# A decoder trunk on one core: retention states in four tiles per burst, gating behind the output product, the last squares as parts of their own

## The chip, the cores and the metric

The kernel runs on one core of a Trainium2 chip. The metric is the time of one execution in device microseconds; it is given as the median of several runs. A profile is one further execution, with its own time beside its span (first to last instruction).

## The reference

One inference step of two decoder layers on 256 prompt tokens and 8 x 4 sample tokens (288 columns), in fp32, model width 2048. Layer 0 mixes by pooling and spatial gating, layer 1 by retention; each is followed by a gated FFN of width 5632 with a causal convolution. A norm stands before and after each sub-layer:

```python
        x = x + rms_norm(m, norm_mix_post[l])
        h = rms_norm(x, norm_ffn_pre[l])
        ...
        x = x + rms_norm(f, norm_ffn_post[l])
```

Retention has 8 heads with a key width of 256 and a value width of 512. For each sample sequence it reads and writes a state of 256 x 512 per head:

```python
        o = jnp.einsum('bhij,bjhe->bihe', sc, vc) + jnp.einsum('bihd,bhde->bihe', qc, S) * xi[None, :, :, None]
        S = g_c[None, :, None, None] * S + jnp.einsum('bjhd,bjhe->bhde', kc * zeta[None, :, :, None], vc)
```

The head's output is normalised, multiplied by a gate silu(h w_g) and put through the output product w_o. The states are outputs too.

## The kernel before

**Weights and products.** All weights come as one stream of 867 chunks of 128 x 1024 (eight blocks of 128 x 128). A chunk is loaded on the SP queue (line 126, tile raw, three buffers), cast by ACT into a high part (L135, whi) and split by DVE into a low part (L144, wlo), four buffers each. A block is used by one group of three matmuls (mm3: L204, L206, L209), with the activations also split into a high and a low part. `product` runs groups over the contracted blocks for each output block and calls an evacuation at its end.

**Side work.** Everything else is written as Python generators in four lists ("evac", "fast", "late", "slow"). After every group `tick` lowers each list's counter by one; at zero the head of the list takes its next step and sets the counter by the number that it yields. So `yield 24` means that the next step is recorded some 24 groups later. The order of every engine's instructions is fixed by this; a list can also be driven to its end at once (`step` in a loop, `drain`).

**Retention.** For head h: `head` (q, k, v products, 128 groups), `gates` (64 groups), and products of the output for earlier heads (`out_part`). When the last v block is evacuated, `units` joins the list "slow". It handles the head's sample states in four bursts n (even or odd sequences, first or second half of the key width), each on four sequences of 128 x 512. A burst loads the states (`load_state`, L873, on SP, one DMA of 1 MB into the single tile s0), and after `yield 24` issues four matmuls of q with the state (L890, qi_ps), in the last burst a product with the own tokens (L893), and four products of k and v (L896, sn_ps). DVE updates the four states (L899), and POOL issues one DMA that stores the tile (L902). The next load follows 16 groups later (12 in the last head) and must wait for that store, since there is one tile. After the last burst the product is normalised (`normed`: statistics on DVE L923 to L415, a power on POOL L417, tile lr, the result "on" on DVE L928), transposed by TensorE (L910, ot_ps), multiplied by gn and the gate, and split into rhi and rlo, the input of `out_part`. `gates` of the next head begins its first evacuation by driving "slow" until the head before it is through.

**Statistics.** `add_out` evacuates the last part of an output product. `squared` squares each of the 16 blocks on ACT; POOL sums blocks 1 to 14 into tile sqm (L322); block 15 stays a part of its own (L408, sqt). `rms_stat` sums each part over the partitions by three small matmuls (L299, st_ps), with keep-warm matmuls (L279) or, in the retention layer, the final prompt state (sf_ps) between the parts. DVE (L302) and POOL (L304) make the factor from it, which is broadcast by TensorE (L313).

## Time and profile before

| | |
|---|---|
| median of 3 runs | 2997.86 us (2996.1 to 2997.89) |
| profiled execution | 2991.17 us, span 2989.4 us |
| busy: PE, weight loads, DVE, ACT, POOL | 99%, 97%, 61%, 40%, 11% of the span |
| mean granted clock | 0.997 |
| DMA | 540.27 MB, mean 181 GB/s |

Busy time says how long an engine had an instruction in it. Waits name the engine or DMA that came last before an instruction could start. PEclk is the granted share of TensorE's 2.4 GHz; 0.50 is 1.2 GHz.

### The profile page before, as it was taken

The numbers are of one execution on the slowest core, as the hardware profiler recorded it, in microseconds if no ns is written. First come the engines' busy times: TensorE is split into PE (matmuls) and PEld (weight loads), VectorE is DVE, ScalarE is ACT, GpSimd is POOL, SyncE is SP. The second block draws the span as 40 slices with busy tenths as digits, with TensorE's granted clock in tenths as the row PEclk, the third lists the DMA queues.
The fourth block names the chain that finished last, engine by engine and source line by source line (L and its number), as shares of the span: only waits on it lengthen the run. The fifth ranks groups of instructions, "written<-read, shape, count | busy, mean of one in ns | idle before, by whom it ended". The sixth has DMA issues, their size and how long they took to land.

```text
span 2989.4 us, 53184 instructions
## 1 busy us (share of the span) xinstructions
PE 2953.1 (99%) x21951; PEld 2890.1 (97%) x21951; DVE 1816.9 (61%) x2699; ACT 1209.7 (40%) x1843; POOL 330.5 (11%) x573
## 2 busy tenths in 40 slices
PE   9999999999999999999999999999999999999998
PEld 9999999999999999989999998998999999999998
DVE  6754864665655657656556565676775565565664
ACT  6344434333333345433333343343643433333334
POOL 3503300000000014000000000000600000000003
PEclk9999999999999999999999999999999999999999
DMA  6544455554555554566757756656445455555553
GB/s 235 161 162 150 159 164 172 162 167 165 163 168 165 163 169 155 193 233 220 243 165 240 248 164 239 229 199 236 160 160 170 163 161 171 162 162 173 161 167 129
DMA packets 159283, 540.27 MB, mean 181 GB/s; under 512 B 15968, under 2 KB 21616, under 8 KB 159040
## 3 DMA queue, kind: packets, MB, share of 16 engines
q1 hardware_dynamic: 146720, 493.45, 50.3%
q0 software_dynamic: 11184, 42.38, 4.3%
q8 instruction: 172, 2.82, 0.4%
q10 hardware_dynamic: 1136, 1.04, 0.1%
q14 instruction: 71, 0.58, 0.1%
HBM read 495.20 MB, written 41.60 MB: 180 GB/s over the span
## 4 chain that ended last, share of the span: by engine, by line
PE 89%; DVE 5%; DMA 3%; ACT 1%; POOL 1%; issue 1%; SPq 0%; DVEq 0%; POOLq 0%; ACTq 0%
PE acc_n L204 27%; PE acc_n L209 26%; PE acc_n L206 26%; DVE wlo L144 2%; DMA s<-in_ret_dram 2%; PE acc_h L209 1%; PE acc_h L204 1%; PE acc_h L206 1%; PE qi_ps L890 1%; DMA out_rets_dram<-s 1%; DVE hl L352 1%; DVE s L899 1%; ACT whi L135 0%; PE sn_ps L896 0%; POOL dbl L514 0%
## 5 line engine op out<-in xcount | busy, mean ns | idle before, releaser
L144 DVE TENSOR_TENSOR wlo<-raw,whi 128x1024 fp32r<-128x1024 f32 (+1 forms) x867 | 1065.3, 1237 | 641.8 <-ACT whi L135 635.7
L204 PE MATMUL acc_n<-hh,whi 128*128 128x288 f32 x4368 | 1302.7, 298 | 0.0
L206 PE MATMUL acc_n<-hl,whi 128*128 128x288 f32 x4368 | 1289.7, 295 | 0.0
L209 PE MATMUL acc_n<-hh,wlo 128*128 128x288 f32 x4368 | 1285.9, 294 | 1.6 <-DVE wlo L144 1.6
L135 ACT CAST whi<-raw 128x1024 fp32r<-128x1024 f32 (+1 forms) x867 | 896.7, 1045 | 841.0 <-PE acc_n L206 585.4
L204 PEld LDWEIGHTS acc_n<-hh,whi 128*128 128x128 f32 x4368 | 819.9, 188 | 6.4 <-issue 4.6
L209 PEld LDWEIGHTS acc_n<-hh,wlo 128*128 128x128 f32 x4368 | 823.3, 188 | 2.2 <-DVE wlo L144 2.1
L206 PEld LDWEIGHTS acc_n<-hl,whi 128*128 128x128 f32 x4368 | 821.1, 188 | 1.4
L204 PE MATMUL acc_n<-fhi,whi 128*128 128x288 f32 x1320 | 389.6, 295 | 0.0
L206 PE MATMUL acc_n<-flo,whi 128*128 128x288 f32 x1320 | 389.5, 295 | 0.0
L209 PE MATMUL acc_n<-fhi,wlo 128*128 128x288 f32 x1320 | 388.8, 295 | 0.0
L209 PEld LDWEIGHTS acc_n<-fhi,wlo 128*128 128x128 f32 x1320 | 248.4, 188 | 0.0
L206 PEld LDWEIGHTS acc_n<-flo,whi 128*128 128x128 f32 x1320 | 247.7, 188 | 0.0
L204 PEld LDWEIGHTS acc_n<-fhi,whi 128*128 128x128 f32 x1320 | 247.4, 187 | 0.0
L632 ACT ACTIVATE gg<-cv 128x256 f32<-128x256 f32 x88 | 36.8, 418 | 372.3 <-DVE cv L630 372.3
L622 POOL COPY co<-fext 128x16 f32<-128x16 f32 x88 | 17.4, 198 | 1419.3 <-DVE fext L620 1419.3
L204 PE MATMUL acc_n<-rhi,whi 128*128 128x288 f32 x496 | 147.4, 297 | 0.0
L206 PE MATMUL acc_n<-rlo,whi 128*128 128x288 f32 x496 | 146.3, 295 | 0.0
L209 PE MATMUL acc_n<-rhi,wlo 128*128 128x288 f32 x496 | 146.2, 295 | 0.0
L899 DVE SCALAR_TENSOR_TENSOR s<-s,sn_ps 128x512 f32<-128x512 f32 x128 | 81.0, 682 | 85.5 <-PE sn_ps L896 85.5
L391 DVE TENSOR_TENSOR mbuf<-mbuf,acc_n 128x288 f32<-128x288 f32 x128 | 57.6, 452 | 113.7 <-PE acc_n L209 113.6
L204 PE MATMUL acc_h<-hh,whi 128*128 128x288 f32 x368 | 109.0, 298 | 1.3 <-ACT whi L135 1.3
(274 smaller groups left out, 2958.9 us busy)
## 6 DMA issues: line engine op xcount, KB each, us to landing
raw<-in_w_dram SPq DMA_DIRECT2D x866, 512.0 KB, 3.6
s<-in_ret_dram SPq DMA_DIRECT2D x32, 1024.0 KB, 6.3
out_rets_dram<-s POOLq DMA_DIRECT2D x32, 1024.0 KB, 5.9
out_retp_dram<-sf POOLq DMA_DIRECT2D x14, 256.0 KB, 2.6
xbuf<-in_x_dram SPq DMA_DIRECT2D x3, 576.0 KB, 6.1
hc<-in_hc_dram SPq DMA_DIRECT2D x8, 177.0 KB, 5.2
out_y_dram<-xbuf SPq DMA_DIRECT2D x3, 288.0 KB, 2.2
out_conv_dram<-co POOLq DMA_DIRECT2D x2, 396.0 KB, 4.1
```

The costliest lines, as they stand in the source:

```text
L135: A.copy(hi[:, a:b], raws[c][:, a:b])
L144: V.tensor_tensor(lo[:, a:b], raw[:, a:b], hi[:, a:b].bitcast(F32), op=ALU.subtract)
L204: PE.matmul(ps, wh, xh, start=start, stop=False)
L206: PE.matmul(ps, wh, xl, start=False, stop=False)
L209: PE.matmul(ps, wl, xh, start=False, stop=stop)
L352: V.scalar_tensor_tensor(hl[k - 2], x[k - 2], col(gain, k - 2), hh[k - 2].bitcast(F32), op0=ALU.mult, op1=ALU.subtract)
L391: V.tensor_tensor(m[:, j, :], m[:, j, :], ps, op=ALU.add)
L622: G.tensor_copy(co[:, f, 0:NB, :], exs[:, :, DS:])
L632: A.activation(g[:, 0:SEQ], c[:, 0:SEQ], AF.Gelu_apprx_tanh)
L890: PE.matmul(pi[32 * g:32 * g + 32, :], qp[:, dt, 32 * b:32 * b + 32], s0[:, g, :], start=n == 0, stop=False, tile_position=(0, 32 * g))
L899: V.scalar_tensor_tensor(s0[:, g, :], s0[:, g, :], g4[h], pns[g], op0=ALU.mult, op1=ALU.add)
```

## The change

The state tile becomes four tiles s0 to s3 of 128 x 512, each with its own load, and its own store as soon as it is updated. The yields change: 20 groups before a head's first burst, 25 before the others (36 in heads 2 and 4), 10 after a burst. The transposes of head h wait until the output product of head h - 2 is recorded. In the statistics, blocks 13, 14 and 15 become parts of their own, in tiles of another tag; the work between parts stands before the last part alone, and without it no keep-warm matmuls stand there.

```diff
--- before.py
+++ after.py
@@ -293,7 +293,7 @@
         zeros = wz.bitcast(F32)
         PE.matmul(ps[0:96, 0:6], zeros[:, 0:96], zeros[:, 0:6], start=True, stop=False)
         for n, sq in enumerate(parts):
-            if n and between:
+            if between and n == len(parts) - 1:
                 between()
             for t in range(3):
                 PE.matmul(ps[0:96, 2 * t:2 * t + 2], sq[:, 96 * t:96 * t + 96], ones[:, 0:2],
@@ -365,7 +365,7 @@
 
     def post_stat(parts, fill=None):
         drain("late")
-        rs = rms_stat(parts, fill[0] if fill else lambda: keep_warm(3))
+        rs = rms_stat(parts, fill[0] if fill else None)
         if fill:
             fill[1]()
         else:
@@ -401,10 +401,10 @@
             if j == 0:
                 parts.append(t288("sqm", tag="sq"))
                 A.activation(parts[0], ps, AF.Square)
-            elif j < KT - 1:
+            elif j < KT - 3:
                 square_add(parts[0], ps, j)
             else:
-                s = t288("sqt", tag="t2")
+                s = t288("sqs", tag="gl")
                 A.activation(s, ps, AF.Square)
                 parts.append(s)
             A.activation(m[:, j, :], ps, AF.Copy, scale=col(gain, j))
@@ -702,7 +702,7 @@
                 return w.rearrange("p t (g c) -> p t g c", c=8)
             return w.rearrange("p (g c) -> p g c", c=8)
         osp = {}
-        rot, tail = [], []
+        rot, tail, projected = [], [], set()
 
         def rope(dst, a, b):
             if not rot:
@@ -846,15 +846,11 @@
                     mm_split(pf, [w[:, jt, 128 * dt:128 * dt + 128] for w in kz], v2[jt], jt == 0, jt == 1)
                 return pf
 
-            last = []
-
             def put_state(dt, pf):
                 if h < HEADS - 1:
                     sf = p1.tile([128, 512], F32, tag="sf", name="sf")
                 else:
-                    if not last:
-                        last.append(p1.tile([128, 4, 512], F32, tag="s0", name="sfl"))
-                    sf = last[0][:, dt, :]
+                    sf = p1.tile([128, 512], F32, tag=f"s{dt}", name="sfl")
                 A.copy(sf, pf)
                 G.dma_start(out=o["retp"][h, 128 * dt:128 * dt + 128, :], in_=sf)
 
@@ -869,25 +865,26 @@
         retsv = o["rets"].rearrange("(g e) h (t p) v -> e h t p g v", e=2, p=128)
 
         def load_state(h, e, dt):
-            s0 = p1.tile([128, 4, 512], F32, tag="s0", name="s0")
-            nc.sync.dma_start(out=s0, in_=retv[e, h, dt])
+            s0 = []
+            for g in range(4):
+                s0.append(p1.tile([128, 512], F32, tag=f"s{g}", name=f"s{g}"))
+                nc.sync.dma_start(out=s0[g], in_=retv[e, h, dt, :, g, :])
             return s0
 
         def units(h, R):
 
 
             qp, km, vs = qpads[h % 2], R["km"], R["vs"]
-            pace = 16 if h < HEADS - 1 else 12
             pi = None
             for n in range(4):
                 e, dt = n % 2, n // 2
                 s0 = load_state(h, e, dt)
-                yield 24
+                yield (36 if h in (2, 4) else 25) if n else 20
                 if pi is None:
                     pi = bank("qi_ps")
                 for g in range(4):
                     b = 2 * g + e
-                    PE.matmul(pi[32 * g:32 * g + 32, :], qp[:, dt, 32 * b:32 * b + 32], s0[:, g, :],
+                    PE.matmul(pi[32 * g:32 * g + 32, :], qp[:, dt, 32 * b:32 * b + 32], s0[g],
                               start=n == 0, stop=False, tile_position=(0, 32 * g))
                 if n == 3:
                     PE.matmul(pi, s2w[h % 2], vs, start=False, stop=True)
@@ -896,14 +893,16 @@
                     PE.matmul(pns[g], km[32 * g:32 * g + 32, e, 128 * dt:128 * dt + 128], vs[32 * g:32 * g + 32, :],
                               start=True, stop=True, tile_position=(32 * g, 0))
                 for g in range(4):
-                    V.scalar_tensor_tensor(s0[:, g, :], s0[:, g, :], g4[h], pns[g], op0=ALU.mult, op1=ALU.add)
+                    V.scalar_tensor_tensor(s0[g], s0[g], g4[h], pns[g], op0=ALU.mult, op1=ALU.add)
+                    G.dma_start(out=retsv[e, h, dt, :, g, :], in_=s0[g])
                     if g == 1:
                         yield 1
-                G.dma_start(out=retsv[e, h, dt], in_=s0)
                 if n == 3:
                     R["on"].append(normed(pi))
-                yield pace
+                yield 10
             on = R["on"]
+            while h >= 2 and h - 2 not in projected:
+                yield 1
             for e in range(4):
                 pt = bank("ot_ps")
                 for t in range(3):
@@ -965,6 +964,7 @@
                 assert step("slow") or ks[-1] in osp
             product([("ret_out", n) for n in ALLK], ks, osp, add_out(heads[0] == 0, parts, "post_mix1"),
                     first=4 if parts is not None else 0)
+            projected.update(heads)
 
         parts = []
         for h in range(HEADS):
```

The order at three places, of before and then of the change.

TensorE at the end of head 0 (qi_ps and sn_ps are the products of a burst, ot_ps the transposes of "on", v_ps a transposed v, acc_n the running product). Before:

```order
L209 MATMUL acc_n<-hh_91,wlo_14263 128x288
L890 MATMUL qi_ps<-s_14308,qpad_12572 32x512 x4
L893 MATMUL qi_ps<-vstk,s2w_12582 128x512
L896 MATMUL sn_ps<-vstk,km 128x512 x4
L910 MATMUL ot_ps<-cst,on 128x128 x12
L204 MATMUL acc_n<-hh_76,whi_14292 128x288
```

Now the burst, and then the place of the transposes:

```order
L887 MATMUL qi_ps<-s_14244,qpad_12572 32x512
L890 MATMUL qi_ps<-vstk,s2w_12582 128x512
L893 MATMUL sn_ps<-vstk,km 128x512 x4
L204 MATMUL acc_n<-hh_77,whi_14254 128x288
...
L807 MATMUL v_ps<-cst,vf 128x128 x2
L808 MATMUL v_ps<-cst,vst_12581 128x128
...
L909 MATMUL ot_ps<-cst,on 128x128 x3
...
L909 MATMUL ot_ps<-cst,on 128x128 x9
L204 MATMUL acc_n<-hh_76,whi_14327 128x288
```

Thirteen groups now stand between the burst and the first three transposes; the other nine follow two groups later, at the place where all twelve stood. From burst to burst it is 39 groups in heads 0, 1, 3, 5, 6 and 7 and 50 in heads 2 and 4; it was 44, and 40 in head 7.

The SP queue around the loads of a burst of head 0 (raw is a weight chunk). Before:

```order
L126 DMA raw_14019<-in_w_dram 128x1024
L873 DMA s_14060<-in_ret_dram 128x4x512
L126 DMA raw_14077<-in_w_dram 128x1024
L126 DMA raw_14127<-in_w_dram 128x1024
L126 DMA raw_14170<-in_w_dram 128x1024
```

Now:

```order
L126 DMA raw_13951<-in_w_dram 128x1024
L871 DMA s_13978<-in_ret_dram 128x512
L871 DMA s_13980<-in_ret_dram 128x512
L871 DMA s_13982<-in_ret_dram 128x512
L871 DMA s_13984<-in_ret_dram 128x512
L126 DMA raw_14015<-in_w_dram 128x1024
```

Four loads stand in the queue ahead of the next weight chunk where one stood.

DVE at the end of head 6 (s is a state tile, bst and mv the statistics of the product). Before:

```order
L727 TENSOR_TENSOR qpad_12574<-qk,hc 128x4x2x4 x2
L144 TENSOR_TENSOR wlo_21516<-raw_21406,whi_21515 128x1024
L899 SCALAR_TENSOR_TENSOR s_21430<-s_21430,sn_ps 128x512 x4
L923 BN_STATS bst_21569<-qi_ps 128x6
L925 BN_AGGR mv_21571<-bst_21569 128x2
L415 TENSOR_SCALAR ve<-mv_21571 128x1
L928 TENSOR_SCALAR on<-qi_ps,mv_21571,lr 128x512
```

Now:

```order
L896 SCALAR_TENSOR_TENSOR s_21594<-s_21594,sn_ps 128x512
L896 SCALAR_TENSOR_TENSOR s_21596<-s_21596,sn_ps 128x512
L144 TENSOR_TENSOR wlo_21691<-raw_21583,whi_21690 128x1024
L896 SCALAR_TENSOR_TENSOR s_21598<-s_21598,sn_ps 128x512
L896 SCALAR_TENSOR_TENSOR s_21600<-s_21600,sn_ps 128x512
L922 BN_STATS bst_21733<-qi_ps 128x6
L924 BN_AGGR mv_21735<-bst_21733 128x2
L415 TENSOR_SCALAR ve<-mv_21735 128x1
L927 TENSOR_SCALAR on<-qi_ps,mv_21735,lr 128x512
```

A weight split now stands between the second and the third update. It is so in heads 3, 5, 6 and 7.

## Rows read from the trace of the kernel before

**Rows 1.** The page, busy time (share of the span) xinstructions of each engine
```profile
PE 2953.1 (99%) x21951; PEld 2890.1 (97%) x21951; DVE 1816.9 (61%) x2699; ACT 1209.7 (40%) x1843; POOL 330.5 (11%) x573
```

**Rows 2.** The waits of TensorE: us in total, times, longest us
```profile
PE qi_ps L890 <- DMA s<-in_ret_dram: 6.4, 7, 1.9
PE ot_ps L910 <- DVE on L928: 5.0, 2, 4.7
...
PE st_ps L299 <- POOL sqm L322: 1.7, 1, 1.7
PE acc_n L209 <- DVE wlo L144: 1.6, 2, 1.0
```

**Rows 3.** The windows: us, busy of PE, PEld, DVE, ACT, POOL; PEclk, DMA share, GB/s
```profile
300.00:1130.00 830.00, 829.32 (x6225) 828.61 (x6224) 494.97 (x684) 330.45 (x453) 60.48 (x161) 1.00 0.52 165
1307.00:1312.00 5.00, 4.92 (x19) 4.63 (x20) 2.93 (x10) 1.30 (x3) 0.00 (x0) 0.50 0.59 195
1605.70:1609.00 3.30, 3.30 (x15) 3.30 (x15) 3.27 (x5) 0.00 (x0) 0.00 (x0) 0.52 0.02 9
2118.00:2124.00 6.00, 5.93 (x36) 5.12 (x37) 1.31 (x4) 1.56 (x4) 2.39 (x5) 1.00 0.31 118
```

**Rows 4.** The timeline of TensorE, end of head 0: start us, us, instruction [idle before]
```profile
1297.66 0.38 PE L807 MATMUL v_ps<-cst,vf 128*128 128x128 f32 x2
...
1300.08 1.07 PE L890 MATMUL qi_ps<-s,qpad 128*32 128x512 f32 x8
...
1301.50 0.50 PE L896 MATMUL sn_ps<-vstk,km 32*128 32x512 f32 x4
...
1307.09 1.33 PE L910 MATMUL ot_ps<-cst,on 128*128 128x128 f32 x5 [4.71 <-DVE on L928]
```

**Rows 5.** The timeline of DVE, the same place
```profile
1298.93 1.22 DVE L144 TENSOR_TENSOR wlo<-raw,whi 128x1024 fp32r<-128x1024 f32 x1
1302.04 2.48 DVE L899 SCALAR_TENSOR_TENSOR s<-s,sn_ps 128x512 f32<-128x512 f32 x4 [1.89 <-PE sn_ps L896]
...
1306.22 0.81 DVE L928 TENSOR_SCALAR on<-qi_ps,mv,lr 128x512 f32<-128x512 f32 x1 [0.68 <-POOL lr L417]
```

**Rows 6.** The timeline of POOL, the same place
```profile
1304.82 0.75 POOL L902 DMA_DIRECT2D out_rets_dram<-s  x1 [18.29 <-DVE s L899]
1305.62 0.56 POOL L417 TENSOR_TENSOR lr<-ve,mhalf 128x1 f32<-128x1 f32 x1
```

**Rows 7.** Lines L873, L902, L859: ns min/median/max of an issue, and its landing
```profile
L873 SPq DMA_DIRECT2D s<-in_ret_dram x32: 378/385/987, 1226.8 to 2067.1; - x32
...
DMA to landing us min/median/max: 5.5/6.3/9.0
...
DMA to landing us min/median/max: 4.7/5.9/8.0
...
L859 POOL DMA_DIRECT2D out_retp_dram<-sf x14: 542/568/613, 1234.7 to 1902.2; - x14
...
DMA to landing us min/median/max: 2.3/2.5/6.2
```

**Rows 8.** The waits of the SP queue: us in total, times, longest us
```profile
SPq L873 <- DMA out_rets_dram<-s: 39.5, 14, 9.0
```

**Rows 9.** The timeline of all engines, the statistic of the first FFN
```profile
1138.79 0.59 PEld L299 LDWEIGHTS st_ps<-ones,sqm 128*96 128x96 f32 x6
...
1139.30 0.54 PEld L279 LDWEIGHTS warm<-wz 128*128 128x128 f32 x3
...
1139.46 0.44 ACT L408 ACTIVATE sqt<-mbuf 128x288 f32<-128x288 f32 x1 [2.44 <-DVE mbuf L394]
...
1139.95 0.66 PEld L299 LDWEIGHTS st_ps<-ones,sqt 128*96 128x96 f32 x6
```

**Rows 10.** The timeline of all engines, the statistic of the retention layer
```profile
2116.02 0.29 PEld L294 LDWEIGHTS st_ps<-wz 128*96 128x96 f32 x2
...
2118.06 0.58 PEld L299 LDWEIGHTS st_ps<-ones,sqm 128*96 128x96 f32 x6 [1.75 <-POOL sqm L322]
```

## The prediction

> **What bounds the kernel now.** I read the page's busy times first: TensorE is busy for 99% of the span [rows 1]. So only two things can shorten the run: less work on TensorE, or fewer of its waits and slow stretches. The change takes away almost no work there: three statistics lose three keep-warm matmuls each, and all four gain six small ones. So the second view is TensorE's waits: state loads cost 6.4 us in seven waits, the transposes behind the normalised product 5.0 us in two, the statistic 1.7 us in one; waits for split weights come to only 1.6 us on that line [rows 2]. These three are what the change touches. Third, the windows with the granted clock: it stands at 0.50 for the 5 us after the longest wait, and at 0.52 for 3.3 us after a wait for a state [rows 3]. 0.50 is the 1.2 GHz level, so half of such a stretch is lost. In a long plain stretch 6225 matmuls take 830 us [rows 3]: 0.133 us each, 0.40 us for the three of a group, which is one step of the side work. I use 0.40 us to turn places in the order into time.
>
> **Part 1: the end of head 0.** Before, the last burst of head 0 is followed at once by all of its twelve transposes, since head 1's first gate forces the side work to its end there. TensorE waits 4.7 us for the tile "on" [rows 2, 4], then runs 5.0 us at half clock [rows 3], which loses 2.5 us: 7.2 us. The wait is a chain: the last state product ends at 1301.50 + 0.50 = 1302.00 [rows 4], then come four updates, the statistics and the power on POOL, and "on" ends at 1306.22 + 0.81 = 1307.03 [rows 5, 6]: 5.03 us. In the new order 13 groups (5.2 us) and a trio of small transposes lie between burst and first gating transposes, because the three periods before it are 39 groups and not 44. 5.2 is over 5.03, so the wait goes and with it the slow clock: -7.2 us. The bound on the other side is 0, if "on" is late for another reason. I take the whole, as the covering work is plain matmuls in fixed order.
>
> **Part 2: state loads and stores in four pieces.** Before, a period is 44 groups, 17.6 us, and a burst of 1.5 us (1.07 for the eight state matmuls, 0.50 for the four products behind them, overlapping a little [rows 4]): 19.1 us. Into it must fit: burst 1.5, updates 2.5 [rows 5], 0.3 to the store's issue (1304.82 less 1304.52) [rows 5, 6], store 5.9, load 6.3 [rows 7]: 16.5 us, and 17.7 where a weight split of 1.22 us [rows 5] stands among the updates. The rest is eaten by the SP queue, where the load stands behind weight loads; 14 of the 32 loads still found the store on its way, 39.5 us in all [rows 8]. So the period is just long enough at the medians, and seven times it was not.
>
> After, a period is 39 groups: 15.6 + 1.5 = 17.1 us (50 groups, 21.5 us, in heads 2 and 4). The slowest piece is the fourth: update ends 4.0 us after the burst's start (5.2 with a weight split), 0.3 to its issue, then a 256 KB store and a 256 KB load. No row has such a piece among three others. The near end is the 256 KB store of the prompt's state, 2.5 us; the far end the worst whole tile, 8.0 for a store and 9.0 for a load [rows 7]. I take 4 us each, nearer to the 256 KB row, since the first three pieces leave earlier: 4.0 + 0.3 + 4 + 4 = 12.3, 13.5 with a split, against 17.1. That leaves 3.6 us for SP. There the load now stands 13 groups (5.2 us) behind the burst instead of 18 or 19, and the weight loads queued behind it wait for the last store; three more issues of 0.385 us [rows 7] add 1.2 us. Those weight loads feed tiles four chunks ahead, and the 1.6 us of waits on split weights [rows 2] show this cover; without it each late us would be one of TensorE. A head's first load stands 21 groups ahead instead of 25: 8.4 us, over the 6.3 median but under the 9.0 worst. For these I keep 1.0 of the 6.4 us: -5.4, and the slow stretch after the 1.9 us wait goes: 3.3 us at 0.52, -1.7. Together -7.1 us (from -8.1, all gone, to the loss of rival 1).
>
> A rule speaks against the pieces. The Trainium skill ("DMA: Bandwidth & Descriptors", section "Anatomy of one DMA") says a DMA costs about 2.0 us fixed plus bytes over 436e3 per us. By it one 1 MB copy takes 4.4 us as an estimate, and four of 256 KB, if each paid in turn, 10.4. The 2.5 us of the 256 KB row agrees with its 2.6 for one piece; whether four overlap no row here shows, and paid in turn they would be rival 1.
>
> **Part 3: transposes closer behind the burst.** Elsewhere 19 groups (15 in head 7) lay between a head's last burst and its transposes; now always 13, 5.2 us. In heads 1, 2 and 4 the chain of 5.03 us fits. In heads 3, 5, 6 and 7 the new order has a weight split between the second and third update: 5.03 + 1.22 = 6.2 us, so TensorE waits 1.0 us in heads 6 and 7, and 0.6 in 3 and 5, where a transposed v (about 0.4 us of TensorE [rows 4]) lies between: 3.2 us. Head 7's old wait, 5.0 - 4.7 = 0.3 [rows 2], goes: +2.9 us. POOL issues four stores, not one, ahead of the power that "on" needs. At 0.57 us, the 256 KB issue [rows 7], the fourth begins 2.8 us after the state products and ends at 3.4, before the power's 3.62 (1305.62 less 1302.00) [rows 6]: nothing. At 0.75, the whole tile's, they run into one another to 4.0 and add 0.4 in each of eight heads. So +0 to +6. The new guard that holds a head's gating until the product two heads back is done delays nothing: the distance is 13 groups in every head, guarded or not.
>
> **Part 4: the last three squares.** In the two FFN statistics and that of layer 0's mixer, the first part's three small matmuls hold the weight port 0.51 us (1138.79 to 1139.30) [rows 9]. Two more parts add 1.02 and end at 1140.32; the last part started at 1139.95 before, right behind its square, which ended at 1139.46 + 0.44 = 1139.90. The keep-warm trio that goes lay under that wait. So +0.37 us, three times: +1.1. In the retention layer the first part waited for POOL's sums until 2118.06 though TensorE was ready at 2116.31 (the zero products of 0.29 from 2116.02); with the last two sums off POOL that is -1.75, and the two parts cost 1.02: -0.7 [rows 10]. Together +0.4 us.
>
> **Sum.** -7.2 - 7.1 + 2.9 + 0.4 = -11.0 us. Against the profiled execution (2991.17 us, of which the span is 2989.4) that is 2980.2. The runs' median lies 6.7 us above that execution; I take the same 11.0 from it: 2986.9 us.
>
> **Rivals.**
> 1. The pieces are as slow as the whole (this is the slower side). The period is now 2 us shorter; if the fourth piece's store and load still take 5.9 + 6.3, the chain is 16.5 to 17.7 us against 17.1, and SP's hold of about 1 us comes on top: 0.4 to 1.6 us of wait in each of the 18 short periods, 7 to 29 us, in place of the old 8.1. Total -7.2 - 8.1 + 2.9 + 0.4 + (7 to 29) = -5 to +17 us, 2993 to 3015. It turns into a loss where the waits pass 12 us in all, 0.67 us a period; by this chain the store and load of the fourth piece must then come to about 11.3 us with a split and 12.5 without. For it: both copies share the engines with the weights, and 14 loads waited for stores [rows 8]. Against: 2.5 us for 256 KB [rows 7], and the early start of three pieces. Chance 0.12.
> 2. The clock falls at the statistics, where the keep-warm trio is gone. Before, the stretch around the retention statistic is at 1.00 although TensorE waited 1.7 us in it [rows 3]. A fall would cost what the two stretches above cost, 1.7 to 2.5 us, at the two statistics that work follows and maybe the third: +3.4 to +7.5, so 2990 to 2994. The Trainium skill ("TensorE: Matmul & The Clock Gate", Part 1) has the clock set by how busy the engine was lately, so that taking filler away invites this. The rows here show falls after waits of 4.7 and 1.9 us and none at the statistic's 1.7, so the trace neither bears it out nor excludes it. Chance 0.12.
> 3. "on" is later than I have it: DVE and POOL are in other work when the burst ends, in most heads, at 1 us more in each: +8, 2995. For it: those engines also carry the splits and evacuations of the running products. Against: before, only head 0 and head 7 waited there at all [rows 2]. Chance 0.11.
> 4. Head 1's forced drain still stalls (nine of its twelve transposes are still issued at the forced place), so the 7.2 us stay: 2994. Against: three go ahead of it. Chance 0.05.
>
> **How the numbers follow.** Forecast 0.60, rivals 0.12, 0.12, 0.11, 0.05. A measurement of this kernel can tell about 0.2%, 6 us, from no change, so faster means below 2991.9. The forecast with its bounds (waits of part 2 all gone and part 3 at 0: 2983; part 3 at its upper end: 2990) lies below that; rival 2 mostly does. Faster: 0.60 + 0.08 = 0.68. Same: rivals 3 and 4, the rest of 2 and half of 1: 0.26. Slower: the upper half of rival 1: 0.06. The range, 2980 to 2996, takes in the forecast's bounds with 3 us for the next run, rivals 2, 3 and 4, and leaves out most of rival 1.
>
> **What would show it.** After: no wait of several us at the transposes of head 0 and the clock at 1.00 there; state waits near 1 us in all; waits of 0.5 to 1 us at the transposes of heads 3, 5, 6 and 7; landing times of the pieces near 4 us; no wait for POOL's sums at the retention statistic, 0.4 us more in each other. The prediction is wrong if pieces land in 6 us or more, if PE's waits for "on" pass 6 us, or if the clock falls at a statistic.

## The result, and the profile after

| | kernel before | changed kernel |
|---|---|---|
| median of the runs side by side | 2994.18 us (6 runs, 2990.11 to 2997.89) | 2979.32 us (6 runs, 2978.10 to 2979.88) |
| ratio, 95% interval | | 0.9949 [0.9937, 0.9962] |
| profiled execution (span) | 2991.17 us (2989.4) | 2978.1 us (2976.3) |

The change is faster by 0.5%. One run of the kernel before, beside experiments 9 to 12, took 5918.56 us and is in no ratio. Three of the six runs of the kernel before are those shown ahead of the prediction (median 2997.86); the other three, taken beside the changed kernel, gave 2990.11 to 2992.27. From profiled execution to profiled execution it is 13.1 us; the forecast's sum was 11.0.

The page, busy time of each engine of the changed kernel:

```profile
PE 2952.5 (99%) x21990; PEld 2890.9 (97%) x21990; DVE 1818.3 (61%) x2699; ACT 1209.7 (41%) x1843; POOL 366.1 (12%) x661
```

TensorE's busy time is where it was [rows 1], 2952.5 us against 2953.1, so nearly all of the 13 us is idle time that went: span less busy time is 23.8 us where it was 36.3. POOL has 35.6 us more, of 96 more DMA issues less the eight sums that went. Next TensorE's waits of the changed kernel, those that stand in [rows 2] and are left:

```profile
PE ot_ps L909 <- DVE on L927: 2.0, 4, 0.7
PE acc_n L209 <- DVE wlo L144: 1.6, 2, 1.0
```

No row for state loads is left (6.4 us in seven waits before). This list has idle time ahead of an instruction; a late piece in the middle of a burst shows instead as a burst that takes longer than its 1.06 us (the first row of head 0 below), and none of the 32 bursts does here. There is no row for POOL's sums at a statistic (1.7 before), and the transposes' wait is 2.0 us in four pieces where it was 5.0 in two. The waits for split weights did not grow. The windows of the changed kernel, with the granted clock in the third column from the right: a plain stretch, the end of head 0, the last statistic.

```profile
300.00:1130.00 830.00, 829.34 (x6225) 828.64 (x6224) 495.49 (x685) 330.10 (x454) 61.51 (x162) 1.00 0.51 165
1300.00:1305.00 5.00, 5.00 (x40) 4.87 (x39) 4.50 (x8) 1.07 (x3) 0.00 (x0) 1.00 0.60 179
...
2960.00:2963.40 3.40, 3.40 (x13) 2.91 (x12) 0.75 (x3) 0.00 (x0) 0.92 (x2) 0.50 0.00 0
```

The plain stretch has 6225 matmuls as in [rows 3]; what changed lies in the retention layer and the statistics. The end of head 0, which ran at 0.50, is at 1.00. The last line is new: at the last statistic the clock stands at 0.50, its 1.2 GHz level, for 3.4 us.

The end of head 0 in the changed kernel, TensorE, then DVE and POOL:

```profile
1293.82 1.06 PE L887 MATMUL qi_ps<-s,qpad 128*32 128x512 f32 x8
...
1295.23 0.51 PE L893 MATMUL sn_ps<-vstk,km 32*128 32x512 f32 x4
...
1301.30 0.49 PE L909 MATMUL ot_ps<-cst,on 128*128 128x128 f32 x3
```

```profile
1295.77 2.48 DVE L896 SCALAR_TENSOR_TENSOR s<-s,sn_ps 128x512 f32<-128x512 f32 x4 [1.31 <-PE sn_ps L893]
...
1299.95 0.81 DVE L927 TENSOR_SCALAR on<-qi_ps,mv,lr 128x512 f32<-128x512 f32 x1 [0.69 <-POOL lr L417]
```

```profile
1296.75 2.33 POOL L897 DMA_DIRECT2D out_rets_dram<-s  x4 [16.30 <-DVE s L896]
1299.35 0.56 POOL L417 TENSOR_TENSOR lr<-ve,mhalf 128x1 f32<-128x1 f32 x1 [0.26 <-DVE ve L415]
```

The state products end at 1295.23 + 0.51 = 1295.74, "on" at 1299.95 + 0.81 = 1300.76: 5.02 us, as before [rows 4 to 6]. The transposes begin at 1301.30, 0.54 us later, with no wait. The four store issues end at 1296.75 + 2.33 = 1299.08, ahead of the power at 1299.35.

Issue (ns, min/median/max) and landing of the state pieces, loads (L871) and stores (L897), and the SP queue's wait at the loads:

```profile
L871 SPq DMA_DIRECT2D s<-in_ret_dram x128: 327/388/1432, 1227.6 to 2048.9; - x128
...
DMA to landing us min/median/max: 3.3/5.1/6.6
...
L897 POOL DMA_DIRECT2D out_rets_dram<-s x128: 539/542/587, 1241.3 to 2061.4; - x128
...
DMA to landing us min/median/max: 2.3/3.0/5.9
```

```profile
SPq L871 <- DMA out_rets_dram<-s: 14.4, 15, 2.4
```

A whole tile's load took 6.3 us and its store 5.9 at the median [rows 7]; a piece's take 5.1 and 3.0. The SP queue's wait for stores fell from 39.5 us, longest 9.0 [rows 8], to 14.4, longest 2.4. By the trace's landing events of all 32 bursts, the last piece lands 0.25 to 7.1 us ahead of its burst, median 3.7; it is less than 1.3 in four of them.

The statistic of the first FFN in the changed kernel, and that of the retention layer behind it:

```profile
1139.35 0.59 PEld L299 LDWEIGHTS st_ps<-ones,sqm 128*96 128x96 f32 x6
...
1139.86 1.61 PEld L299 LDWEIGHTS st_ps<-ones,sqs 128*96 128x96 f32 x18
...
1139.95 0.44 ACT L408 ACTIVATE sqs<-mbuf 128x288 f32<-128x288 f32 x1 [2.45 <-DVE mbuf L394]
...
1145.30 0.40 PE L204 MATMUL acc_h<-hh,whi 128*128 128x288 f32 x1
...
2102.30 0.59 PEld L299 LDWEIGHTS st_ps<-ones,sqm 128*96 128x96 f32 x6
...
2102.82 1.10 PEld L299 LDWEIGHTS st_ps<-ones,sqs 128*96 128x96 f32 x12
```

At the first FFN the three parts follow the first without a gap. In the retention layer the first part follows the zero products at once; its 1.75 us of wait [rows 10] are gone. Measured from the start of the last matmul of the product to the first matmul of the next (to the broadcast of the result for the last one), the four statistics took 5.85, 5.86, 8.37 and 3.35 us before and take 6.15, 6.17, 7.58 and 4.08 after.

### The profile page after: what moved, and what is told of

The parts are those of the page before. It is cut to its first block, busy times and chain, and to the rows that moved or that the text cites. A ratio compares the mean times of both kernels' runs of the same rounds, so it can differ in the third digit from the quotient of the medians.

```text
span 2976.3 us, 53668 instructions
## 1 busy us (share of the span) xinstructions
PE 2952.5 (99%) x21990; PEld 2890.9 (97%) x21990; DVE 1818.3 (61%) x2699; ACT 1209.7 (41%) x1843; POOL 366.1 (12%) x661
## 4 chain that ended last, share of the span: by engine, by line
PE 93%; DVE 4%; ACT 1%; issue 1%; POOL 1%; DMA 0%; SPq 0%; DVEq 0%; POOLq 0%; ACTq 0%
PE acc_n L204 28%; PE acc_n L209 28%; PE acc_n L206 28%; DVE wlo L144 2%; PE acc_h L209 1%; PE acc_h L204 1%; PE acc_h L206 1%; PE qi_ps L887 1%; DVE hl L352 1%; PE sn_ps L893 0%; POOL dbl L514 0%; DVE pn L380 0%; PE st_ps L299 0%; DVE s L896 0%; PE ot_ps L909 0%
## 5 line engine op out<-in xcount | busy, mean ns | idle before, releaser
L897 POOL DMA_DIRECT2D out_rets_dram<-s x128 | 69.4, 542 | 412.7 <-DVE s L896 405.4
```

Source lines behind the costliest of these rows:

```text
L897: G.dma_start(out=retsv[e, h, dt, :, g, :], in_=s0[g])
```

## The experiments

All ratios are to the kernel before, run on the same chip; experiments 1 to 4 shared one chip, 5 to 8 another, 9 to 12 a third. The change itself was run side by side with the kernel before (median 2979.32 us) and in experiment 5 (2978.78); no run of it stands beside experiments 1 to 4 or 9 to 12. The kernel before gave medians of 2991.21, 2991.73 and 2990.09 us in the three groups, so a median may be compared across groups to 1 or 2 us.

### 1. The kernel before, once more

No edit. It tells how large the run-to-run scatter of the base is.

> The kernel before, unchanged, to see how its time, its waits for state loads and its clock spread. Theory A (the first three runs, near 2997, held more or longer waits for state loads, with slow-clock stretches behind them, than the profiled execution with its 6.4 us of such waits): the runs lie between 2989 and 2998, and the ones that take longer show a lower mean clock, by about 0.001 for each 3 us (a 3.4 us stretch at half clock is 0.0006 of the span, and the wait ahead of it is as long); the profile shows the 4.7 us wait at the end of head 0 and between 4 and 13 us of waits for state loads. Rival B (a part of the time that no engine's waits show, such as the launch, differs from session to session): the clock is the same in all runs, and the difference between time and span moves with the time.

Measured: 2991.68 us (11 runs, 2988.6 to 2993.65) beside 2991.21 (28 runs, 2986.94 to 2994.6); ratio 1.0004 [0.9996, 1.0013]. Its profiled execution took 2992.37 us with a span of 2990.7, so 1.7 lie around the span, as in the profile before (2991.17 - 2989.4 = 1.8). The 2996 to 2998 of the three runs ahead of the prediction did not come back here (one single run beside experiments 9 to 12 took 2996.89). Its waits for states were 4.5 us in six, and the wait at the end of head 0 was 4.7 again.

The record has the mean granted clock of 56 runs of this kernel in experiments 1 to 12. The longer a run, the lower its clock: 2987.7 us on average at 0.998 (4 runs), 2989.6 at 0.997 (19), 2991.9 at 0.996 (29) and 2994.3 at 0.995 (4). That is about 2.2 us for each 0.001, where theory A had 3. Between 1.65 and 1.78 us lie around the span in all of them. So theory A holds in this and rival B does not: the scatter lies within the span.

The base of this kernel is 2990 to 2992, and the 6.7 us by which the median shown lay above the profiled execution were not a property of the kernel; what made them is not settled.

### 2. The change with one tile and one store per burst

The rest of the change (yields, guard, statistic) stays.

```diff
-            s0 = []
-            for g in range(4):
-                s0.append(p1.tile([128, 512], F32, tag=f"s{g}", name=f"s{g}"))
-                nc.sync.dma_start(out=s0[g], in_=retv[e, h, dt, :, g, :])
+            s0 = p1.tile([128, 4, 512], F32, tag="s0", name="s0")
+            nc.sync.dma_start(out=s0, in_=retv[e, h, dt])
...
-                    G.dma_start(out=retsv[e, h, dt, :, g, :], in_=s0[g])
                     if g == 1:
                         yield 1
+                G.dma_start(out=retsv[e, h, dt], in_=s0)
```

> The changed kernel with one state tile again (one load, one store of 1 MB), all else as in the change, the yields and with them the order of TensorE included. Theory A (pieces are needed for periods of 39 groups): the chain burst, updates, store 5.9, load 6.3 is 16.5 to 17.7 us against a period of 17.1, with SP's hold on top, so state loads are waited for 7 to 29 us in all, in most of the 18 short periods, and the clock falls behind some: 2988 to 3012, 9 us or more over the change. Rival B (the shorter distance to the gating alone made the gain, the pieces nothing): within 3 us of the change, 2976 to 2982, waits for state loads under 3 us.

Measured: 2984.31 us (11 runs, 2981.72 to 2993.24), ratio 0.9985 [0.9976, 0.9994]. By medians it lies 5.0 to 5.5 us above the change, nearer to rival B's 3 than to theory A's 9; by the ratios 8 to 11. Its runs scatter over 11.5 us, those of the change over 1.8. Its profiled execution was the slowest of its eleven (2993.24), so the waits below are the upper end; the median run, 9 us shorter, left no profile. TensorE's waits there, then the landing of its loads and the SP queue's wait:

```profile
PE qi_ps L889 <- DMA s<-in_ret_dram: 8.8, 6, 3.3
PE ot_ps L911 <- DVE on L929: 2.9, 4, 1.2
```

```profile
DMA to landing us min/median/max: 5.3/6.1/8.3
```

```profile
SPq L873 <- DMA out_rets_dram<-s: 73.4, 24, 6.3
```

With one tile the shorter periods bring the waits for states back, six of them with 8.8 us in this execution, and 24 loads wait 73.4 us for stores. So it is the four tiles that keep the period of 39 groups free of such waits. But by its median this version is still 6.9 us faster than the kernel before: more than half of the gain comes without the four tiles.

### 3. The old distances with four tiles

```diff
-                yield (36 if h in (2, 4) else 25) if n else 20
+                yield 24
...
-                yield 10
+                yield 16 if h < HEADS - 1 else 12
```

> The changed kernel with the yields of before (24 ahead of every burst, 16 behind it, 12 in the last head); four tiles and the new statistics stay. Theory A: all of head 0's transposes stand right behind its last burst again, so the wait of about 4.7 us and the half clock behind it (2.5 us) come back, the waits of 2.0 us for the normalised product in heads 3, 5, 6 and 7 go to 0.3, and the waits for state loads stay at 0 with 44 groups: about +5.5 us to the change, 2983 to 2987. Rival B (the pieces brought nothing, the periods did): waits for state loads return with 4 us or more, 2989 to 2995.

Measured: 2986.82 us (11 runs, 2983.72 to 2988.56), ratio 0.9987 [0.9979, 0.9996]: 7.5 to 8 us above the change by medians, and the upper end of what was expected (5.5). Its waits at the transposes, and the SP queue's at the loads:

```profile
PE ot_ps L909 <- DVE on L927: 5.0, 2, 4.7
```

```profile
SPq L871 <- DMA out_rets_dram<-s: 7.1, 4, 4.8
```

No row for states is in the list, but three bursts were held inside by a late piece, 2.0 us in all. The longest of them, to be read beside the 1.06 us of a burst in the changed kernel:

```profile
1843.50 2.32 PE L887 MATMUL qi_ps<-s,qpad 128*32 128x512 f32 x8
```

Head 0's end costs what it cost before. So Part 1 needs the distances and Part 2 the tiles, but the two are not quite separate: at the old distances four tiles still leave 2.0 us of late pieces, which the expected 5.5 did not have.

### 4. The change with the old statistic

```diff
-            elif j < KT - 3:
+            elif j < KT - 1:
...
-                s = t288("sqs", tag="gl")
+                s = t288("sqt", tag="t2")
```

and the three keep-warm matmuls and their place as before.

> The changed kernel with the statistics of before: blocks 13 and 14 summed on POOL again, three keep-warm matmuls between the parts. Theory A (the new parts gain 0.8 us in the retention statistic and lose 0.3 in each of the other three, 0.4 more in the last where the clock fell): 0.5 us less than the change, that is no difference, 2977 to 2981; the wait of 1.7 us for POOL's sum is back in the retention statistic, each other statistic is 0.3 us shorter, and the clock does not fall at the last statistic. Rival B (the statistics carry a good part of the gain): 3 us or more over the change.

Measured: 2980.33 us (6 runs, 2977.39 to 2983.37), ratio 0.9963 [0.9951, 0.9975], 1.0 above the change. That is within theory A's range, and the new statistic gives nothing that these runs resolve. The profiled execution was the slowest of the six. Two of its bursts were held by late pieces, 1.1 us in all, though tiles and distances are those of the change: their reserve is not whole in every execution. Also in it the wait for POOL's sums is back, and behind it the clock fell for 6.8 us:

```profile
PE st_ps L299 <- POOL sqm L322: 1.7, 1, 1.7
```

```profile
2107.50:2114.30 6.80, 6.80 (x23) 5.58 (x23) 0.16 (x1) 1.17 (x2) 1.43 (x2) 0.50 0.17 64
```

### 5. The changed kernel, once more

No edit; the base for experiments 6 to 8.

> The changed kernel, unchanged, for its spread and as the base of the runs beside it. Theory A (the change made the kernel insensitive to how long a state transfer takes): 2977 to 2982 on any chip, no wait for a state load, while the kernel before lies anywhere between 2987 and 2998. Rival B (the change is as sensitive, and its earlier runs were lucky): single runs scatter by 6 us or more and the profile shows waits for state loads.

Measured: 2978.78 us (5 runs, 2978.57 to 2979.49), before beside it 2991.73 (9 runs, 2986.59 to 2993.56), ratio 0.9959 [0.9945, 0.9972]. By these medians the change is worth 12.95 us.

### 6 and 7. The loads of a head's later bursts 1.6 us later, before and after

Four groups are moved from behind the load to ahead of it, so that TensorE's order and the distance from burst to burst stay. Before (6) and the change (7):

```diff
-                yield 24
+                yield 20 if n else 24
...
-                yield pace
+                yield pace if n == 3 else pace + 4
```

```diff
-                yield (36 if h in (2, 4) else 25) if n else 20
+                yield (32 if h in (2, 4) else 21) if n else 20
...
-                yield 10
+                yield 10 if n == 3 else 14
```

> The kernel before with the loads of a head's second to fourth burst placed four groups (1.6 us) later, at 20 groups ahead of the burst and not 24; the order on TensorE is the same. It imitates state transfers that take 1.6 us longer. Theory A (its loads have no slack, so transfers that take longer on a chip are paid in full): the loads that a store does not already hold back are late by up to 1.6 us more; waits for state loads rise from 4.5 to 6.4 us to 12 to 25, with further stretches at half clock: 5 to 20 us over the kernel before, 2996 to 3011. Rival B (SP's hold behind weight loads decides, not the place): within 3 us of the kernel before.

> The changed kernel with the same shift: the loads of a head's second to fourth burst four groups (1.6 us) later, 21 groups ahead of the burst and not 25 (32 and not 36 in heads 2 and 4); the order on TensorE is the same. Theory A (the pieces have slack): in its trace the last piece landed 0.2 to 7.1 us ahead of its burst, under 1.6 us in five of the 24 places; a shift of 1.6 us then makes waits of about 3 us in all, 1.4 at the longest: 0 to 4 us over the change. Rival B (no slack either): 6 us or more over the change.

Measured: before 3010.09 us (5 runs, 3008.11 to 3012.08), ratio 1.0062 [1.005, 1.0075], 18.4 above the kernel before. The change 2980.74 (5 runs, 2979.59 to 2982.65), ratio 0.9964 [0.9952, 0.9977], 2.0 above experiment 5. Both are what theory A expects. The waits for states in 6; and one of three bursts of 7 (two in head 0, one in head 1) that a late piece held inside:

```profile
PE qi_ps L890 <- DMA s<-in_ret_dram: 16.5, 13, 2.8
```

```profile
1278.14 1.52 PE L887 MATMUL qi_ps<-s,qpad 128*32 128x512 f32 x8
```

The old chain had no reserve: 1.6 us later made thirteen waits of 16.5 us out of seven of 6.4, and its trace has three stretches at half clock in the retention layer besides that at the end of head 0 (3.4, 6.8 and 6.8 us), where the first profile has one. The new one has 1.6 us of reserve in all but five of the 32 bursts (four of the 24 that the shift moves, where the expectation says five), by the change's landing events, although its period is 2 us shorter in 18 of 24 places. The three bursts in 7 took 2.2 us longer than they do unheld, which is the 2.0 that it lost; the list of waits has no row for them.

### 8. A mixed version

The new statistic in the retention layer alone, the other three as before; the last burst's transposes three groups later in the heads where "on" came late.

```diff
-        rs = rms_stat(parts, fill[0] if fill else None)
+        rs = rms_stat(parts, fill[0] if fill else lambda: keep_warm(3))
...
-            elif j < KT - 3:
+            elif j < (KT - 3 if gain == "post_mix1" else KT - 1):
...
-                yield 10
+                yield 13 if n == 3 and h in (3, 5, 6, 7) else 10
```

> The changed kernel with two things put back or moved: the new parts of the statistic in the retention layer alone (the other three statistics as before, with their keep-warm matmuls), and the transposes of heads 3, 5, 6 and 7 three groups (1.2 us) further behind the last burst. Theory A (by the stage times: 0.3 us back in each of three statistics and the clock stays up at the first and last of them, waits of 2.0 us for the normalised product go): 3 us less than the change, 2974 to 2978, the clock at 1.00 from 20 us to the end of the last statistic, waits for the normalised product under 0.5 us. Rival B (the clock at the statistics falls by chance, whatever stands between the parts): within 1.5 us of the change, with a stretch at half clock at one of the statistics.

Measured: 2974.14 us (5 runs, 2974.05 to 2974.69), ratio 0.9943 [0.993, 0.9955]: 4.6 below the change, as theory A expects, so it beats both kernels. No wait for "on" is left. Its statistics take 5.86, 5.86, 7.58 and 3.34 us. The windows of its four parts of the span:

```profile
16.00:300.00 284.00, 280.77 (x2102) 278.45 (x2102) 167.35 (x240) 133.01 (x209) 89.45 (x98) 1.00 0.51 170
300.00:1130.00 830.00, 829.30 (x6225) 828.60 (x6224) 496.44 (x687) 330.78 (x454) 60.67 (x161) 1.00 0.51 165
1130.00:2130.00 1000.00, 997.38 (x7368) 943.28 (x7367) 654.00 (x1072) 410.45 (x721) 157.42 (x238) 1.00 0.63 214
2130.00:2962.00 832.00, 830.26 (x6225) 828.47 (x6223) 485.88 (x678) 325.43 (x444) 55.08 (x158) 1.00 0.50 162
```

The clock is at 1.00 in all four.

### 9 to 12. The mixed version taken apart

Experiment 9 has only the two statistic edits of 8, experiment 10 only the later transposes, experiment 12 is 8 again. Experiment 11 is the change with the keep-warm trio put back (the first edit of 8 alone), all statistics in four parts.

> The change with its new statistic kept in the retention layer alone; the other three statistics as before (one sum for the first parts, three keep-warm matmuls). Theory A (the 4.6 us by which the mixed version beat the change are a sum of a statistic's part and a gating part): the three statistics give back 0.30 + 0.31 + 0.73 = 1.3 us, the waits for the tile on (2.0 us) stay: the change less 1.3, 2977 to 2978 where the change is 2979, and the clock stays up at the last statistic. Theory B (the new statistic costs more than its own path, through the clock): the change less 2.5 or more, 2976.5 or less.

> The change with the transposes of heads 3, 5, 6 and 7 three groups (1.2 us) later, all else as in the change. Theory A: the 2.0 us of waits for the tile on go, nothing else moves: the change less 2.0, about 2977, and the clock still falls at the last statistic. Theory B (nearly all of the mixed version's gain is of the statistics): the change less 0 to 1. Theory C (TensorE's waits in these heads cost more than the profile shows as waits): the change less 3 or more.

> The change with the three keep-warm matmuls put back ahead of the last part in three statistics; the parts stay four. Theory A (the fall of the clock at the last statistic comes from the keep-warm trio that went): no stretch at half clock there, and the trio lies under the wait for the last square or adds up to 0.3 us each: within 1 us of the change. Theory B (the fall comes from the parts, whose small matmuls hold the port for longer): the clock still falls there to half for about 3 us; within 1 us of the change or above it by up to 1.5.

> The mixed version again, beside its two halves. Theory A (its gain over the change is the sum of a statistic's part and a gating part): it lies below the statistic's half by what the gating's half gains, and below the gating's half by what the statistic's half gains, to 1 us; 2974 to 2975.5. Theory B (one of the halves does it all): it lies within 0.7 us of one of them.

| | median us (5 runs each) | range | ratio, 95% interval |
|---|---|---|---|
| 9, statistic alone | 2977.70 | 2976.6 to 2978.58 | 0.9958 [0.9945, 0.9971] |
| 10, gating alone | 2976.63 | 2974.28 to 2979.15 | 0.9953 [0.9938, 0.9968] |
| 11, parts and keep-warm | 2980.18 | 2979.29 to 2981.26 | 0.9967 [0.9954, 0.998] |
| 12, mixed again | 2974.94 | 2973.41 to 2975.17 | 0.9948 [0.9935, 0.996] |

The mixed version lies 2.8 us below 9, which is the gating's worth, and 1.7 below 10, the statistic's worth (1.3 us by the stage times, 0.4 of it the clock). Both halves count, and they add: theory A of these runs. Experiment 10 lies 2.2 to 2.7 below the change, nearer to theory A's 2.0 than to theory C's 3. But by the starts of TensorE's instructions the four waits cost 2.9 us and not the 2.0 of the list (Part 3 below), so theory C's mechanism is there too. One detail of theory A missed: in the profile of experiment 10 the clock did not fall at the last statistic but at the first. In experiment 9 the last statistic runs at full clock again:

```profile
2950.00:2968.00 18.00, 13.68 (x96) 12.36 (x94) 6.99 (x15) 2.81 (x6) 7.17 (x8) 1.00 0.19 70
```

Experiment 11 answers its question in one execution only. With the trio back the clock stayed up at the last statistic, as theory A says; that the trio did it is not shown, since the clock also stayed up there in experiment 10 without it. At the first statistic, which neither theory speaks of, it fell:

```profile
289.10:292.50 3.40, 3.40 (x13) 2.92 (x13) 0.16 (x1) 0.00 (x0) 1.67 (x5) 0.51 0.22 51
```

The trio, which lay under the wait for the last square before, has no cover behind three parts:

```profile
1142.59 1.10 PEld L299 LDWEIGHTS st_ps<-ones,sqs 128*96 128x96 f32 x12
1143.61 0.54 PEld L279 LDWEIGHTS warm<-wz 128*128 128x128 f32 x3
1144.18 0.73 PEld L299 LDWEIGHTS st_ps<-ones,sqs 128*96 128x96 f32 x6
```

The last part starts at 1144.18, 1.59 us after the two before it; in the changed kernel the three follow in one go. At the first FFN that is 0.7 us more than the change by TensorE's starts. The parts and the trio together are the dearest form.

## Why the prediction was right or wrong

The direction was right and the mechanisms were: every wait named in Parts 1, 2 and 4 went. Of its own signs of being wrong one came in full, the clock fell at a statistic (the last); of another there were single cases, load pieces that took up to 6.6 us at a median of 5.1. The time, 2979.3 us, lies 7.6 us below the forecast and 0.7 below the low end.

**The step that failed** is the last of the sum: "The runs' median lies 6.7 us above that execution; I take the same 11.0 from it". The kernel before ran at 2990 to 2992 us everywhere else: 2991.07 (the median of the three runs beside the change), 2991.21, 2991.73 and 2990.09 in the experiments. These lie within about 1 us of the profiled execution, 2991.17, so the 6.7 should have been about 0. The sum against the profiled execution, which the text also gives, was 2980.2; the measured time is 0.9 below it. So most of the miss is a base of three runs, all high, to which a difference from another execution was applied; its range allowed 3 us below the forecast's bounds, less than the 6.7 us by which the base was off.

The rest is in the sizes of the terms, of which Part 2 was the one too small:

- **Part 1, -7.2: right.** No wait at head 0's transposes, clock 1.00 for the 5 us behind them, "on" 5.02 us behind the products (forecast 5.03). Experiment 3 shows the 4.7 us wait whole when the distances alone are put back.
- **Part 2, -7.1: under-sized, -8.1.** The 1.0 us kept for states that still come late was 0. The chain itself is longer than I had it: from a burst's start to the last landing of the next burst's pieces it takes 14.2 to 17.0 us, median 15.0, where I added 12.3 (13.5 with a split) and left 3.6 for SP. With one tile at the same distances (experiment 2) it takes 15.6 to 20.5, median 16.7. The fourth store takes 4.3 us at the median (forecast 4), a load piece 5.1 (forecast 4). As a set the pieces are no faster than the whole tile: from the first issue to the last landing four stores take 6.3 us and four loads 7.2 at the median, against 5.9 and 6.3. But these do not stand end to end: the first load leaves, at the median, 0.8 us before the fourth store has landed, because it needs the first tile alone. One burst of head 1 had only 0.25 us left. Experiments 6 and 7 show the reserve, 2 that the tiles make it.
- **Four copies do not pay in turn.** The first store piece of a burst lands after 2.3 us at the median. That agrees with the 2.6 that the Trainium skill's rule gives ("DMA: Bandwidth & Descriptors", section "Anatomy of one DMA"). The section is on copies issued from GpSimd (POOL), which here are the stores; the prediction put the loads, which SP issues, under it too. Paid in turn, four stores would take 10.4 us by it, as an estimate; they took 6.3 at the median (4.8 to 8.9). Four loads took 7.2 (5.9 to 8.1). So the copies of a set overlap. Rival 1 was right that a set takes as long as the whole tile, and wrong in putting its store and load end to end.
- **Part 3, +2.9: about right, +2.4.** "On" came 6.2 us behind the products in heads 3, 5, 6 and 7, as forecast, because of the weight split between the second and third update. The list of waits has 2.0 us in these four heads where I had 3.2, because I let the whole trio wait, and only its third transpose waits for the new tile. But what a wait costs is more than its idle time. Head 6 in the changed kernel, then the same place in experiment 8, where nothing waits:

```profile
1945.72 0.38 PE L909 MATMUL ot_ps<-cst,on 128*128 128x128 f32 x2
1946.78 0.33 PE L909 MATMUL ot_ps<-cst,on 128*128 128x128 f32 x1 [0.67 <-DVE on L927]
1946.86 0.38 PE L204 MATMUL acc_n<-hh,whi 128*128 128x288 f32 x1
```

```profile
1946.39 0.49 PE L909 MATMUL ot_ps<-cst,on 128*128 128x128 f32 x3
1946.63 0.38 PE L204 MATMUL acc_n<-hh,whi 128*128 128x288 f32 x1
```

  From the first transpose to the next group it is 1.14 us instead of 0.24: 0.90 lost for 0.67 listed. Over heads 3, 5, 6 and 7 it is 0.55, 0.55, 0.90 and 0.90, 2.9 us in all; head 7's old wait, 0.27 listed, cost 0.5. Why "on" is late in head 6, on DVE:

```profile
1941.74 1.22 DVE L144 TENSOR_TENSOR wlo<-raw,whi 128x1024 fp32r<-128x1024 f32 x1
...
1945.91 0.81 DVE L927 TENSOR_SCALAR on<-qi_ps,mv,lr 128x512 f32<-128x512 f32 x1 [0.75 <-POOL lr L417]
```

  POOL's four issues cost nothing, as said. The guard moves nothing: from the last burst to the first transposes it is 7.1 to 7.5 us in every head.
- **Part 4, +0.4: right, +0.55.** +0.30 and +0.31 where +0.37 was forecast, -0.79 for -0.7 in the retention layer, and +0.73 at the last one, of which 0.4 is the clock. The half clock cost another 0.5 us behind that statistic: the last output lands 13.4 us after the broadcast begins, and 12.9 in experiment 10, where the clock did not fall there.

With the 2.0 - 0.3 = 1.7 of the list for Part 3, the terms add to -7.2 - 8.1 + 1.7 + 0.55 = -13.05, against 13.1 measured between the two executions. That this fits to 0.1 us is luck. From the last matmul of the product ahead of the first FFN's statistic to that of the product ahead of the retention layer's statistic the time fell from 977.4 to 963.0 us, by 14.5, where these terms (with the first FFN's +0.31) make 13.3. The difference was paid back in places that the terms leave out: 0.3 us ahead of the first statistic and 0.9 behind the last one, the 0.5 of the clock among it. Of what the sum lacks in the retention layer, two waits of the running head's own products are a share: those for qk and vth stood in the list with 0.5 and 0.4 us before and have no row after.

The experiments, which take one thing away with the rest in place, give other sizes again: by medians the tiles are worth 5.0 to 5.5 us (experiment 2), the distances 7.5 to 8 (experiment 3) and the statistic 1.0 (experiment 4), where the prediction's sum had 7.1, 7.2 - 2.9 = 4.3, and -0.4.

**The rivals.** Rival 1 did not come. Rival 2 came in part, at one statistic in each of the two executions of the change, and cost about 0.9 us (0.4 and 0.5, above) and not 1.7. Rival 3 (1 us more in most heads) did not come: 0.5 to 0.9 in the four heads that Part 3 names. Rival 4 did not come.

**What stays open** is what made the three runs ahead of the prediction 5 to 7 us longer. Falls of the clock differ from one execution to the next (below), and longer runs have the lower clock (experiment 1), but the record has neither a profile nor the clock of those three runs.

## What to carry to other kernels

Cutting a tile that is loaded, updated in place and stored into parts with buffers of their own shortens the chain from use to next use, here to a median of 15.0 us where one tile at the same distances takes 16.7: the next load's first part needs the first store only. The distance from a product to the reader of its result must be set together with that, and for each place by itself, since a piece of other work in between (a weight split of 1.22 us) decides whether 5.2 us suffice. And a forecast of a small difference is best stood on the profiled execution it was read from, with the spread of the base as part of the range.

## What the runs showed of the hardware that was not expected

The granted clock falls at statistics in some executions and not in others, in stretches of 3.4 or 6.8 us at 0.50 (1.2 GHz). Over the fourteen profiled executions:

- At the retention statistic with the old form, where TensorE waits 1.7 us for POOL and then issues small products: in 3 of 4 (experiments 1, 4 and 6, not the first profile). By TensorE's starts this costs 1.6 to 3.2 us. With the four-part form: in none of 10. This gain of the change, -0.8 in the two profiles compared, is therefore up to 4 us in others. Experiment 1:

```profile
2119.00:2125.80 6.80, 6.80 (x24) 5.79 (x23) 1.83 (x6) 1.93 (x4) 2.69 (x7) 0.50 0.21 78
```

- At the first statistic with the old form: in none of 7; with four parts in 5 of 7 (experiments 2, 3, 7, 10 and 11), at about 1.3 us each, but in neither execution of the change itself, although experiments 2, 3, 7 and 10 differ from it only behind that statistic.
- At the last statistic with the old form or the trio put back: in none of 8; with four parts and no trio in 5 of 6.
- At the statistic of the first FFN, in none of 14.

The page counts TensorE as busy in all these stretches (6.80 of 6.80 us above), so busy time does not tell them; ahead of them TensorE had waited for POOL (retention) or issued the small products of three or four parts in a row (the first and the last). The Trainium skill ("TensorE: Matmul & The Clock Gate", Part 1) has the clock follow how busy the engine was lately; the counts here agree with it in sign at the retention statistic, where the wait that went took the falls with it, and at the last, where filler went and falls came. At the first the clock fell with the filler back in place too (experiment 11). And at the same statistic of the same kernel the clock fell in one execution and stood in another (the old retention statistic, 3 of 4), so neither the place nor the order of work fixes it.
